# RWKV mixing: a PSUM copy of h as second operand of the mixes, and low parts of the key inputs by turns

## The chip, the cores and the metric

The kernel runs on one core of one Trainium2 chip. The metric is the device time of one execution in microseconds (us). PE is TensorE (matmuls), DVE is VectorE, ACT is ScalarE, POOL is GpSimd, SP is SyncE, which here only issues DMAs. SBUF is the working memory of the engines, PSUM the memory into which PE writes; DVE and ACT read and write both.

## What is computed

Two layers of a generator with 512 latent tokens and 256 context tokens of 1024 channels. Layer 0 mixes tokens by neighbourhood attention, layer 1 by bidirectional RWKV-7; each is followed by 16 experts. The change lies at the start of the RWKV layer, where every token's vector `h` is mixed with the mean of its two neighbours, with six learned vectors, one for each product that follows:

```
def centred_shift(h):
    hp = jnp.pad(h, ((0, 0), (1, 1), (0, 0)))
    return 0.5 * (hp[:, :-2] + hp[:, 2:])
xx = centred_shift(h) - h
x_s = h + xx * mix[s]          # s = receptance, decay, key, value, iclr, gate (0..5)
r, k, v = x_0 @ w_r, x_2 @ w_k, x_3 @ w_v
decay, iclr, gate: low-rank products, x_1 @ w1, x_4 @ a1, x_5 @ g1, each followed by a second one
```

(The last three lines are the reference's, shortened to their shape.)

## The kernel before

`rw_inputs` first norms the rows and turns them, so that channels lie on the 128 partitions: `hh` holds for each of 8 channel blocks `k` 772 columns (512 latent and 256 context tokens with zero columns between), all float32 in SBUF. A loop over the 8 blocks then does the mixing. For a block, `shifted(k)` makes `xx`: POOL adds the left and the right neighbour (`q` is POOL's queue, line 1069), DVE halves and subtracts `h` (line 1070). `mix(s, k)` makes one mixed input: one DVE instruction, `xx` times a column of `mixT` plus `h` (line 1079); or, with `spread`, a scaled copy on ACT and an add of `h` on POOL (lines 1076 and 1077). Six mixes are made for a block:

- 1 (decay) and 4 (iclr), 770 columns, for the low-rank products on PE (line 1117), whose sums lie in PSUM in `ph`;
- 2 (key), 770 columns: `part` splits it for the three-pass products into a rounded high part `xah` (ACT, line 947) and the rest `xal` (line 948, on POOL for blocks 0 to 6, on DVE for block 7);
- 5 (gate), 512 columns, for line 1119;
- 0 (receptance), 512 columns on DVE, and 3 (value), 770 columns by the spread way, tile name `md`; both go to DRAM (`xmd`, lines 1126 and 1127) and are loaded again later.

On the way PE also forms the keys of the first three token tiles (lines 1123 to 1125, sums in `pk`). Then `lora` and three copies empty the PSUM tiles on ACT and DVE, and a woven stage follows: products of keys and receptances on PE (lines 260 to 262) and `rw_keys`, then the values, then the scan over the tokens, then routing and the experts.

PSUM has 8 banks: 3 of the pool `mm`, 2 of `tp`, 3 of `ps_k0` here. The order of each engine's instructions in this part is set when the kernel is built, by a scheduler that plays the program through and takes the instructions as they come ready; each engine then runs its list strictly in order. The scan's order is written out by hand.

Of the kernel before, what the change touches and what calls it, by code (L numbers as in the profile page):

```python
# [20 lines left out]
F32 = mybir.dt.float32  # L21
# [984 lines left out]
def rw_inputs(S, pool):  # L1006

    nc, I, tc = S.nc, S.I, S.tc
    q = nc.gpsimd
# [15 lines left out]
    with tc.tile_pool(name="rwn", bufs=1) as xn:  # L1025
# [11 lines left out]
        hp = S.rwk.enter_context(tc.tile_pool(name="rwh", bufs=1, side="right"))  # L1037
# [28 lines left out]
    S.wraw = left.enter_context(tc.tile_pool(name="rwwr", bufs=2, reuse_waits="tile"))  # L1066

    def shifted(k):
        q.tensor_tensor(xx[:, k], hh[:, k, 0:770], hh[:, k, 2:772], op=ALU.add)
        nc.vector.scalar_tensor_tensor(xx[:, k], xx[:, k], 0.5, hh[:, k, 1:771], op0=ALU.mult, op1=ALU.subtract)  # L1070

    def mix(s, k, n=770, tag="mx", spread=False):
        t = wl.tile([P, 770], F32, name=tag, bufs=MXB[tag])[:, :n]
        m = mixT[:, 8 * s + k:8 * s + k + 1]
        if spread:
            nc.scalar.activation(t, xx[:, k, :n], AF.Copy, scale=m)
            q.tensor_tensor(t, t, hh[:, k, 1:n + 1], op=ALU.add)
        else:
            nc.vector.scalar_tensor_tensor(t, xx[:, k, :n], m, hh[:, k, 1:n + 1], op0=ALU.mult, op1=ALU.add)
        return t  # L1080

    def lora(ps, hid, fn):
        for z in range(2):
            for p, c0, n in ps:
                hs, h1 = (h[:, c0:c0 + n] for h in hid[z])
                t = wl.tile([64, 512], F32, name="ht")[:, :n]
                nc.scalar.activation(t, p[64 * z:64 * z + 64, :n], fn)
                nc.vector.tensor_copy(hs[0:64], t)
                nc.vector.tensor_copy(h1[0:64], t)
                nc.vector.tensor_tensor(hs[64:128], t, hs[0:64].bitcast(F32), op=ALU.subtract)  # L1090

    def weights(name, n):
        return split_weights(S, wp, "w", [(0, I[name][0][:, n * 256:(n + 1) * 256])], 3)

    xk = halves(xsp, "xa", 770)
    ready, S.ks = {}, [[None] * (NT // 2) for n in range(4)]
    with tc.tile_pool(name="rwl", bufs=2, reuse_waits="tile") as wl, tc.tile_pool(name="ps_k0", bufs=3, space=PSUM) as ps0:
        lw = []
        for name in ("rw_w1", "rw_a1"):
            w = wl.tile([P, KD, 2, 64], F32, name="lw", bufs=3)  # L1100
            for z in range(2):
                q.dma_start(w[:, :, z, :], I[name][0, z].rearrange("(k p) r -> p k r", p=P))
            lw.append(w.rearrange("p k z r -> p k (z r)"))
        lw.append(wl.tile([P, KD, P], F32, name="lw", bufs=3))
        q.dma_start(lw[2], I["rw_g1"][0].rearrange("(k p) r -> p k r", p=P))
        w0 = weights("rw_w_k", 0)
        ph = [[(p.tile([P, 512], F32, name=n), c0, w) for c0, w in ((0, 512), (512, 256))]
              for p, n in ((S.ps_tp, "tp"), (S.ps_mm, "mm"))]
        pg = S.ps_mm.tile([P, 512], F32, name="mm")
        pk = [ps0.tile([P, 256], F32, name="k0") for _ in range(3)]  # L1110
        for k in range(KD):
            shifted(k)
            on = dict(start=(k == 0), stop=(k == KD - 1))
            for i, s in enumerate((1, 4)):
                t = mix(s, k)
                for p, c0, n in ph[i]:
                    nc.tensor.matmul(p[:, :n], lw[i][:, k], t[:, at(c0 // P):at(c0 // P) + n], **on)
            part(S, xk, k, mix(2, k), q if k < LOQ else nc.vector)
            nc.tensor.matmul(pg, lw[2][:, k], mix(5, k, SEQ), **on)
            for t in range(3):  # L1120
                s = slice(t * P, (t + 1) * P)
                (xh, xl), (wh, wll) = (x[:, k, s] for x in xk), w0(k)
                nc.tensor.matmul(pk[t], xh, wh, start=(k == 0), stop=False)
                nc.tensor.matmul(pk[t], xh, wll, start=False, stop=False)
                nc.tensor.matmul(pk[t], xl, wh, start=False, stop=(k == KD - 1))
            nc.sync.dma_start(S.xmd[0][k], mix(0, k, SEQ, "md"))
            nc.sync.dma_start(S.xmd[1][k], mix(3, k, tag="md", spread=k < SPREAD))
        lora(ph[0], hidW, AF.Tanh)
        lora(ph[1], hidA, AF.Copy)
        nc.scalar.activation(S.hidG, pg, AF.Tanh, scale=0.5)  # L1130
        nc.vector.tensor_scalar(S.hidG, S.hidG, 0.5, 0.5, op0=ALU.mult, op1=ALU.add)
        base.close()
        S.kp = S.rwk.enter_context(tc.tile_pool(name="rwkst", bufs=2, side="right", reuse_waits="tile"))

        def key_tile(n, t):
            if t % 2 == 0:
                S.ks[n][t // 2] = S.kp.tile([P, 2, 256], F32, name="ks", bufs=KSB)
# [24 lines left out]


MXB = {"mx": 5, "md": 2}
SPREAD, LOQ, KSB, BOOST = 8, 7, 6, 1000
KSTART, KRATE = 0, 1.75


# [777 lines left out]
```

## Time and profile before

| | us |
|---|---|
| median of 3 runs | 2755.37 |
| their range | 2753.96 to 2766.93 |
| profiled execution, its own time | 2758.18 |
| its span, first to last instruction | 2756.4 |
| mixing loop in it, about | 1304 to 1374 |

Over the span PE is busy 90%, DVE 48%, ACT 36%, POOL 21%. These are means over stages with different limits: in the loop that the change touches DVE has next to no idle time, in the stages behind it PE is the busy one, and in the last third the loads of the experts' weights keep the DMA engines full. The page's chain that ended last follows those weights back through the last 320 us. So a reading of the loop must go by its own stretch. [...]

### The profile page before, as it was taken

The numbers are of one execution on the slowest core, as the hardware profiler recorded it, in microseconds if no ns is written. First come the engines' busy times: TensorE is split into PE (matmuls) and PEld (weight loads), VectorE is DVE, ScalarE is ACT, GpSimd is POOL, SyncE is SP. The second block draws the span as 40 slices with busy tenths as digits, with TensorE's granted clock in tenths as the row PEclk, the third lists the DMA queues.
The fourth block names the chain that finished last, engine by engine and source line by source line (L and its number), as shares of the span: only waits on it lengthen the run. The fifth ranks groups of instructions, "written<-read, shape, count | busy, mean of one in ns | idle before, by whom it ended". The sixth has DMA issues, their size and how long they took to land. (4 is left out here: it accounts for less than half of the span.)

```text
span 2756.4 us, 44025 instructions
## 1 busy us (share of the span) xinstructions
PE 2470.2 (90%) x16800; PEld 1574.1 (57%) x16800; DVE 1327.1 (48%) x3006; ACT 1004.0 (36%) x2127; POOL 591.5 (21%) x857
## 2 busy tenths in 40 slices
PE   6998999898999999997698697999999977998887
PEld 4876879793333333333388686777777862332222
DVE  6665566642222222225978845666666771221222
ACT  3555556642111101113266634766665431000100
POOL 2100000121000000001656525665655110000000
PEclk9999999998999999998899898999999978999999
DMA  8646440328787878784157866565554369999998
GB/s 246 147 150 187 132 152 15 109 100 327 298 320 312 334 305 329 293 357 172 69 186 241 269 167 130 124 134 125 126 122 125 87 243 378 420 420 421 420 420 342
DMA packets 378371, 637.64 MB, mean 231 GB/s; under 512 B 133832, under 2 KB 301056, under 8 KB 329008
## 3 DMA queue, kind: packets, MB, share of 16 engines
q1 hardware_dynamic: 370944, 609.11, 63.5%
q0 software_dynamic: 7216, 25.70, 2.5%
q8 instruction: 134, 2.20, 0.3%
q14 instruction: 77, 0.63, 0.1%
HBM read 565.11 MB, written 53.88 MB: 225 GB/s over the span
## 5 line engine op out<-in xcount | busy, mean ns | idle before, releaser
L790 PE MATMUL P<-wm,xin 128*64 128x512 f32 x2048 | 494.3, 601 | 25.8 <-DMA wm<-in_moe_w_dram 24.7
L790 PEld LDWEIGHTS P<-wm,xin 128*64 128x64 f32 x2048 | 141.0, 137 | 328.3 <-issue 259.4
L823 PE MATMUL mm<-wm,hidT 128*64 128x512 f32 x1024 | 245.9, 601 | 16.8 <-ACT hidT L807 14.9
L801 ACT ACTIVATE hid<-P 128x512 f32<-128x512 f32 x32 | 19.1, 597 | 563.3 <-PE P L790 563.3
L763 POOL DMA_INDIRECT xg<-xnd,ii x20 | 19.7, 985 | 846.5 <-PE tp L77 571.5
L837 DVE SCALAR_TENSOR_TENSOR Y<-mm,gates,gt 64x512 f32<-64x512 f32 x64 | 48.0, 750 | 283.1 <-PE mm L823 282.4
L260 PE MATMUL mm<-wh,hTh 128*128 128x256 f32 x576 | 173.5, 302 | 1.9 <-ACT hTh L554 1.9
L802 DVE TENSOR_TENSOR hid<-P,hid 128x512 f32<-128x512 f32 x32 | 22.1, 692 | 308.3 <-PE P L790 293.6
L262 PE MATMUL mm<-wh,hTl 128*128 128x256 f32 x576 | 168.4, 293 | 1.9 <-DVE hTl L557 1.9
L261 PE MATMUL mm<-wl,hTh 128*128 128x256 f32 x576 | 168.7, 293 | 0.0
L823 PEld LDWEIGHTS mm<-wm,hidT 128*64 128x64 f32 x1024 | 72.7, 137 | 151.9 <-issue 121.3
L1477 POOL TENSOR_TENSOR Wi<-Wi,Ti 112x30 f32<-112x30 f32 (+14 forms) x240 | 141.4, 589 | 18.8
L1475 POOL TENSOR_TENSOR Ti<-Wi 112x30 f32<-112x30 f32 (+14 forms) x240 | 134.9, 562 | 18.2
L795 PE MATMUL Pc<-wm,xin 128*32 128x512 f32 x1024 | 138.5, 597 | 0.0
L260 PEld LDWEIGHTS mm<-wh,hTh 128*128 128x128 f32 x576 | 114.3, 199 | 11.9 <-issue 8.8
L262 PEld LDWEIGHTS mm<-wh,hTl 128*128 128x128 f32 x576 | 113.6, 198 | 4.5 <-DVE hTl L557 2.8
L1554 PE MATMUL mm<-FR,QF 128*128 128x128 f32 (+1 forms) x768 | 115.1, 294 | 0.4 <-ACT QF L1542 0.4
L261 PEld LDWEIGHTS mm<-wl,hTh 128*128 128x128 f32 x576 | 114.6, 199 | 1.3 <-issue 1.1
L864 DVE TENSOR_TENSOR X<-mm,X 128x512 f32<-128x512 f32 x80 | 52.6, 687 | 111.9 <-PE mm L863 111.7
L1554 PEld LDWEIGHTS mm<-FR,QF 128*128 128x128 f32 x768 | 98.7, 200 | 7.4 <-ACT QF L1542 0.9
L1542 ACT ACTIVATE QF<-mm 64x256 f32<-64x256 f32 x192 | 72.6, 378 | 67.7 <-PE mm L1538 64.3
L1557 DVE TENSOR_TENSOR FT<-mm,eye 64x128 f32<-64x128 f32 x192 | 55.8, 292 | 78.9 <-ACT FT L1556 76.6
(437 smaller groups left out, 5715.6 us busy)
## 6 DMA issues: line engine op xcount, KB each, us to landing
wm<-in_moe_w_dram SPq DMA_DIRECT2D x378, 1024.0 KB
adaw<-in_ada_w_dram SPq DMA_DIRECT2D x96, 512.0 KB
wraw<-in_na_w_qkv_dram SPq DMA_DIRECT2D x32, 256.0 KB
wm<-in_moe_w_dram POOLq DMA_DIRECT2D x6, 1024.0 KB, 10.8
pkd<-sig SPq DMA_DIRECT2D x24, 256.0 KB
pkd<-kka SPq DMA_DIRECT2D x24, 256.0 KB
pkd<-av SPq DMA_DIRECT2D x24, 256.0 KB
sig<-pkd SPq DMA_DIRECT2D x16, 384.0 KB
```

What stands on the lines that cost most here:

```text
L260: S.nc.tensor.matmul(ps, xh, wh, start=(k == 0), stop=False)
L261: S.nc.tensor.matmul(ps, xh, wl, start=False, stop=False)
L262: S.nc.tensor.matmul(ps, xl, wh, start=False, stop=(k == n - 1))
L790: nc.tensor.matmul(ps[64 * hf:64 * hf + 64], xin[:, k, cl], w[:, hf * 512:(hf + 1) * 512], start=k == 0, stop=k == KD - 1)
L795: nc.tensor.matmul(Pc[32 * i:32 * i + 32], xinc[:, k, cc], ws[k][i // 2][:, (i % 2) * 512:(i % 2 + 1) * 512], start=k == 0, stop=k == KD - 1)
L823: nc.tensor.matmul(py[64 * hf:64 * hf + 64], hT[:, k % 4, k // 4, :], ws[k][:, hf * 512:(hf + 1) * 512], start=k == 0, stop=k == KD - 1)
L864: nc.vector.tensor_tensor(X[t][:, sl], ps, X[t][:, sl], op=ALU.add)
L1475: nc.gpsimd.tensor_tensor(t, W3[:, i + 1:32, i:i + 1].to_broadcast([112, n, i]), W3[:, i:i + 1, 0:i].to_broadcast([112, n, i]), op=ALU.mult)
L1477: nc.gpsimd.tensor_tensor(W3[:, i + 1:32, 0:i], W3[:, i + 1:32, 0:i], t, op=ALU.add)
L1542: nc.scalar.activation(QF[m][0:64, u], pq[64 * u:64 * u + 64], AF.Copy)
L1554: nc.tensor.matmul(pf[:, h, s0:], QF[m][:, u, h, :], rhs, start=True, stop=True)
L1557: nc.vector.tensor_tensor(F[64:128, :, 64:128], pf[64:128, :, 64:128], S.eye2[64:128, None, :].to_broadcast([64, 2, 64]), op=ALU.add)
```

## The change

For each block ACT copies `h` from `hh` to a PSUM tile `hp` (line 1072 of the changed kernel). DVE's subtract (line 1073) and its five mixes (line 1083) read `hp` in place of `hh`. The spread mix reads `hh` as before, and is now the first of a block. The low part `xal` is made on DVE for even blocks and on POOL for odd ones (line 1130).

To make room, `hp` takes 2 banks, and there is one such tile; `ps_k0` keeps one bank for one key tile. The other two key tiles share a bank of `mm`, and the two 256-column ends of the low-rank sums share a bank of `tp`; of the sums that share a bank only the first begins with `start`.

```diff
     def shifted(k):
+
         q.tensor_tensor(xx[:, k], hh[:, k, 0:770], hh[:, k, 2:772], op=ALU.add)
-        nc.vector.scalar_tensor_tensor(xx[:, k], xx[:, k], 0.5, hh[:, k, 1:771], op0=ALU.mult, op1=ALU.subtract)
-
-    def mix(s, k, n=770, tag="mx", spread=False):
+        hp = ps0.tile([P, 1024], F32, name="hp")[:, :770]
+        nc.scalar.activation(hp, hh[:, k, 1:771], AF.Copy)
+        nc.vector.scalar_tensor_tensor(xx[:, k], xx[:, k], 0.5, hp, op0=ALU.mult, op1=ALU.subtract)
+        return hp
+
+    def mix(s, k, hp, n=770, tag="mx", spread=False):
...
-            nc.vector.scalar_tensor_tensor(t, xx[:, k, :n], m, hh[:, k, 1:n + 1], op0=ALU.mult, op1=ALU.add)
+            nc.vector.scalar_tensor_tensor(t, xx[:, k, :n], m, hp[:, :n], op0=ALU.mult, op1=ALU.add)
...
-    with tc.tile_pool(name="rwl", bufs=2, reuse_waits="tile") as wl, tc.tile_pool(name="ps_k0", bufs=3, space=PSUM) as ps0:
+    with tc.tile_pool(name="rwl", bufs=2, reuse_waits="tile") as wl, tc.tile_pool(name="ps_k0", bufs=1, space=PSUM) as ps0:
...
-        ph = [[(p.tile([P, 512], F32, name=n), c0, w) for c0, w in ((0, 512), (512, 256))]
-              for p, n in ((S.ps_tp, "tp"), (S.ps_mm, "mm"))]
+        pc = S.ps_tp.tile([P, 2, 256], F32, name="tp")
+        ph = [[(S.ps_tp.tile([P, 512], F32, name="tp"), 0, 512), (pc[:, 0], 512, 256)],
+              [(S.ps_mm.tile([P, 512], F32, name="mm"), 0, 512), (pc[:, 1], 512, 256)]]
         pg = S.ps_mm.tile([P, 512], F32, name="mm")
-        pk = [ps0.tile([P, 256], F32, name="k0") for _ in range(3)]
+        pk = S.ps_mm.tile([P, 2, 256], F32, name="mm")
+        pk = [pk[:, 0], pk[:, 1], ps0.tile([P, 256], F32, name="k0")]
         for k in range(KD):
-            shifted(k)
+            hp = shifted(k)
...
+            nc.sync.dma_start(S.xmd[1][k], mix(3, k, hp, tag="md", spread=True))
...
-            part(S, xk, k, mix(2, k), q if k < LOQ else nc.vector)
-            nc.tensor.matmul(pg, lw[2][:, k], mix(5, k, SEQ), **on)
+            t = mix(2, k, hp)
+            nc.scalar.activation(xk[0][:, k], t, AF.Copy)
+            nc.tensor.matmul(pg, lw[2][:, k], mix(5, k, hp, SEQ), **on)
+            nc.sync.dma_start(S.xmd[0][k], mix(0, k, hp, SEQ, "md"))
+            (q if k % 2 else nc.vector).tensor_tensor(xk[1][:, k], t, xk[0][:, k].bitcast(F32), op=ALU.subtract)
...
-            nc.sync.dma_start(S.xmd[0][k], mix(0, k, SEQ, "md"))
-            nc.sync.dma_start(S.xmd[1][k], mix(3, k, tag="md", spread=k < SPREAD))
```

The scheduler gives the engines other lists with it. DVE's list at the loop's start, before, from the first `xx`: `xx` is a block's shift, `mx` and `md` are its mixes (`out<-in`, partitions x columns).

```order
L1070 SCALAR_TENSOR_TENSOR xx<-xx,hh 128x770
L253 TENSOR_TENSOR wl<-wraw,wh 128x1024
L1079 SCALAR_TENSOR_TENSOR mx<-xx,mixT,hh 128x770 x3
L1079 SCALAR_TENSOR_TENSOR mx<-xx,mixT,hh 128x512
L1079 SCALAR_TENSOR_TENSOR md<-xx,mixT,hh 128x512
L1070 SCALAR_TENSOR_TENSOR xx<-xx,hh 128x770 x4
L1079 SCALAR_TENSOR_TENSOR mx<-xx,mixT,hh 128x770 x2
L1079 SCALAR_TENSOR_TENSOR md<-xx,mixT,hh 128x512
```

And DVE's list of the change at the same place, through blocks 0, 1 and the first half of 2.

```order
L1073 SCALAR_TENSOR_TENSOR xx<-xx,hp 128x770
L253 TENSOR_TENSOR wl<-wraw,wh 128x1024
L1083 SCALAR_TENSOR_TENSOR mx<-xx,mixT,hp 128x770 x3
L1083 SCALAR_TENSOR_TENSOR mx<-xx,mixT,hp 128x512
L1083 SCALAR_TENSOR_TENSOR md<-xx,mixT,hp 128x512
L1130 TENSOR_TENSOR xal<-mx,xah 128x770
L1073 SCALAR_TENSOR_TENSOR xx<-xx,hp 128x770
L1083 SCALAR_TENSOR_TENSOR mx<-xx,mixT,hp 128x770 x3
L1083 SCALAR_TENSOR_TENSOR mx<-xx,mixT,hp 128x512
L1083 SCALAR_TENSOR_TENSOR md<-xx,mixT,hp 128x512
L1073 SCALAR_TENSOR_TENSOR xx<-xx,hp 128x770
```

The shifts no longer run ahead of the mixes: a block is now one shift and five mixes, and an even block has its low part behind them.

ACT's list in the loop, before (`md` the scaled copy of the spread mix, `xah` the high part of the key input):

```order
L1076 ACTIVATE md<-xx,mixT 128x770
L947 ACTIVATE xah<-mx 128x770
L1076 ACTIVATE md<-xx,mixT 128x770
L947 ACTIVATE xah<-mx 128x770
L1076 ACTIVATE md<-xx,mixT 128x770
```

And ACT's list of the change there:

```order
L1080 ACTIVATE md<-xx,mixT 128x770
L1127 ACTIVATE xah<-mx 128x770
L1072 ACTIVATE hp<-hh 128x770
L1080 ACTIVATE md<-xx,mixT 128x770
L1127 ACTIVATE xah<-mx 128x770
L1072 ACTIVATE hp<-hh 128x770
```

The copy `hp` of a block stands behind the scaled copy and the high part of the block before it.

The third place is ACT's list behind the loop, where the sums are emptied. Before (`ht` empties a low-rank sum, `hidG` the gate's, `ks` a key tile):

```order
L1087 ACTIVATE ht<-tp 64x512
L1130 ACTIVATE hidG<-mm 128x512
L1087 ACTIVATE ht<-tp 64x256
L1087 ACTIVATE ht<-mm 64x512
L1076 ACTIVATE md<-xx,mixT 128x770
L1087 ACTIVATE ht<-mm 64x256
L1087 ACTIVATE ht<-mm 64x512
L1087 ACTIVATE ht<-mm 64x256
L1140 ACTIVATE ks<-k_10871 128x256
```

And of the change, from the copies `w2s` of the next stage's weights on:

```order
L1230 ACTIVATE w2s<-wraw 64x1024 x2
L1139 ACTIVATE hidG<-mm 128x512
L1091 ACTIVATE ht<-tp 64x512
L1091 ACTIVATE ht<-tp 64x256
L1149 ACTIVATE ks<-mm 128x256 x2
L1149 ACTIVATE ks<-k_10871 128x256
L1220 ACTIVATE krows<-krows 128x256
L1234 ACTIVATE w_11357<-wraw 1x1024 x2
L1158 ACTIVATE ks<-mm 128x256
```

The key copies now come before the low-rank sums of the pool `mm`, and two copies of weights before `hidG`. Behind this stage the scan's lists are the same.

## Rows read from the trace of the kernel before

**Rows 1.** Stretches: us, busy PE, PEld, DVE, ACT, POOL (instructions); clock, DMA share, GB/s.

```profile
1304.00:1384.00 80.00, 50.78 (x181) 30.72 (x179) 78.49 (x71) 20.54 (x28) 48.77 (x23) 0.84 0.19 70
1384.00:1590.00 206.00, 171.26 (x1288) 165.05 (x1289) 158.92 (x205) 131.84 (x224) 114.68 (x114) 0.91 0.75 237
1590.00:2212.00 622.00, 571.84 (x4406) 488.14 (x4405) 402.73 (x1072) 358.41 (x891) 318.00 (x532) 0.95 0.55 124
2435.00:2756.00 321.00, 271.48 (x1170) 92.29 (x1168) 70.70 (x117) 27.07 (x53) 3.75 (x4) 0.99 0.97 404
```

**Rows 2.** Chain that ended last, its first long DMA piece: start, us, what.

```profile
2435.40 21.12 DMA wm<-in_moe_w_dram
```

**Rows 3.** Timeline, SP's issues of the last layer's expert weights: start, us, what.

```profile
2232.82 96.23 SPq L645 DMA_DIRECT2D wm<-in_moe_w_dram  x38
```

**Rows 4.** DVE's groups by shape, 1300 to 1376 us: busy us, mean ns.

```profile
L1079 DVE SCALAR_TENSOR_TENSOR mx<-xx,mixT,hh 128x770 f32<-128x770 f32 x24 | 37.9, 1615 | 0.0
L1070 DVE SCALAR_TENSOR_TENSOR xx<-xx,hh 128x770 f32<-128x770 f32 x8 | 11.0, 1417 | 0.0
L1079 DVE SCALAR_TENSOR_TENSOR md<-xx,mixT,hh 128x512 f32<-128x512 f32 x7 | 10.6, 1513 | 0.0
L1079 DVE SCALAR_TENSOR_TENSOR mx<-xx,mixT,hh 128x512 f32<-128x512 f32 x8 | 7.1, 890 | 0.0
```

**Rows 5.** Instructions that read or write `hh`: ns least/median/most, first and last start.

```profile
L1079 DVE SCALAR_TENSOR_TENSOR mx<-xx,mixT,hh x32: 736/1009/2591, 1310.0 to 1371.8; 128x770 f32<-128x770 f32 x24, 128x512 f32<-128x512 f32 x8
L1069 POOL TENSOR_TENSOR xx<-hh x8: 1459/2181/2447, 1303.8 to 1317.8; 128x770 f32<-128x770 f32 x8
L1070 DVE SCALAR_TENSOR_TENSOR xx<-xx,hh x8: 948/949/2558, 1305.9 to 1332.5; 128x770 f32<-128x770 f32 x8
```

**Rows 6.** DVE's timeline in the loop: start, us, what, idle before.

```profile
1329.12 1.01 DVE L1079 SCALAR_TENSOR_TENSOR mx<-xx,mixT,hh 128x770 f32<-128x770 f32 x1
1331.59 1.82 DVE L1070 SCALAR_TENSOR_TENSOR xx<-xx,hh 128x770 f32<-128x770 f32 x2
...
1372.83 0.96 DVE L948 TENSOR_TENSOR xal<-mx,xah 128x770 fp32r<-128x770 f32 x1 [0.25 <-ACT xah L947]
...
1377.89 0.73 DVE L1079 SCALAR_TENSOR_TENSOR md<-xx,mixT,hh 128x512 f32<-128x512 f32 x1
```

**Rows 7.** POOL's timeline at the loop's start.

```profile
1303.75 15.92 POOL L1069 TENSOR_TENSOR xx<-hh 128x770 f32<-128x770 f32 x8 [10.11 <-ACT hh L1063]
```

**Rows 8.** DVE adds with one operand in PSUM, near the scan's end: least/median/most.

```profile
L1715 DVE TENSOR_TENSOR acc<-mf,acc x64: 411/425/426, 2117.8 to 2229.2; 128x256 f32<-128x256 f32 x64
```

**Rows 9.** Timeline there, POOL and DVE at the same time.

```profile
2156.21 2.52 POOL L1694 TENSOR_TENSOR fraw<-fraw,rgate 128x512 f32<-128x512 f32 x2 [6.39 <-DMA fraw<-in_rw_w_o_dram]
2156.26 0.42 DVE L1715 TENSOR_TENSOR acc<-mf,acc 128x256 f32<-128x256 f32 x1 [0.61 <-PE mf L262]
...
2157.56 0.42 DVE L1715 TENSOR_TENSOR acc<-mf,acc 128x256 f32<-128x256 f32 x1 [0.60 <-PE mf L262]
```

**Rows 10.** A DVE instruction of the mixes' kind, `mm` in PSUM: busy us, mean ns.

```profile
L837 DVE SCALAR_TENSOR_TENSOR Y<-mm,gates,gt 64x512 f32<-64x512 f32 x64 | 48.0, 750 | 283.1 <-PE mm L823 282.4
```

**Rows 11.** ACT's groups, 1300 to 1376 us: busy us, mean ns, idle before.

```profile
L947 ACT ACTIVATE xah<-mx 128x770 fp32r<-128x770 f32 x8 | 6.8, 846 | 51.1 <-DVE mx L1079 51.1
L1076 ACT ACTIVATE md<-xx,mixT 128x770 f32<-128x770 f32 x7 | 6.5, 935 | 3.2 <-DMA xmd<-md 1.8 <-DVE xx L1070 1.4
```

**Rows 12.** PE's timeline behind the loop: start, us, what, idle before and its releaser.

```profile
1377.57 0.39 PE L260 MATMUL mm<-wh,xah 128*128 128x256 f32 x1 [2.74 <-ACT hidG L1130]
...
1385.37 0.58 PE L260 MATMUL mm<-wh,xah 128*128 128x256 f32 x1 [3.18 <-ACT ht L1087]
```

**Rows 13.** Timeline: SP's issue of two `xmd` stores, and ACT behind them.

```profile
1320.25 9.31 SPq L1126 DMA_DIRECT2D xmd<-md  x2
...
1331.32 0.94 ACT L1076 ACTIVATE md<-xx,mixT 128x770 f32<-128x770 f32 x1 [0.30 <-DMA xmd<-md]
```

**Rows 14.** ACT's timeline behind the loop, two copies of weights: start, us, what.

```profile
1387.16 2.14 ACT L1221 ACTIVATE w2s<-wraw 64x1024 fp32r<-64x1024 f32 x2
```

More of the change, by code (lines that the diff above doesn't have):

```diff
@@ L1106, in rw_inputs @@
         w0 = weights("rw_w_k", 0)
-        ph = [[(p.tile([P, 512], F32, name=n), c0, w) for c0, w in ((0, 512), (512, 256))]
-              for p, n in ((S.ps_tp, "tp"), (S.ps_mm, "mm"))]
+        pc = S.ps_tp.tile([P, 2, 256], F32, name="tp")
+        ph = [[(S.ps_tp.tile([P, 512], F32, name="tp"), 0, 512), (pc[:, 0], 512, 256)],
+              [(S.ps_mm.tile([P, 512], F32, name="mm"), 0, 512), (pc[:, 1], 512, 256)]]
         pg = S.ps_mm.tile([P, 512], F32, name="mm")
-        pk = [ps0.tile([P, 256], F32, name="k0") for _ in range(3)]
+        pk = S.ps_mm.tile([P, 2, 256], F32, name="mm")
+        pk = [pk[:, 0], pk[:, 1], ps0.tile([P, 256], F32, name="k0")]
         for k in range(KD):
-            shifted(k)
+            hp = shifted(k)
             on = dict(start=(k == 0), stop=(k == KD - 1))
+            nc.sync.dma_start(S.xmd[1][k], mix(3, k, hp, tag="md", spread=True))
             for i, s in enumerate((1, 4)):
-                t = mix(s, k)
+                t = mix(s, k, hp)
                 for p, c0, n in ph[i]:
-                    nc.tensor.matmul(p[:, :n], lw[i][:, k], t[:, at(c0 // P):at(c0 // P) + n], **on)
-            part(S, xk, k, mix(2, k), q if k < LOQ else nc.vector)
-            nc.tensor.matmul(pg, lw[2][:, k], mix(5, k, SEQ), **on)
+                    nc.tensor.matmul(p[:, :n], lw[i][:, k], t[:, at(c0 // P):at(c0 // P) + n],
+                                     start=k == 0 and (i == 0 or c0 == 0), stop=k == KD - 1 and (i == 1 or c0 == 0))
+            t = mix(2, k, hp)
[3 more added lines that the diff above has]
+            (q if k % 2 else nc.vector).tensor_tensor(xk[1][:, k], t, xk[0][:, k].bitcast(F32), op=ALU.subtract)
             for t in range(3):
@@ L1122, in rw_inputs @@
                 (xh, xl), (wh, wll) = (x[:, k, s] for x in xk), w0(k)
-                nc.tensor.matmul(pk[t], xh, wh, start=(k == 0), stop=False)
+                nc.tensor.matmul(pk[t], xh, wh, start=(k == 0 and t != 1), stop=False)
                 nc.tensor.matmul(pk[t], xh, wll, start=False, stop=False)
-                nc.tensor.matmul(pk[t], xl, wh, start=False, stop=(k == KD - 1))
-            nc.sync.dma_start(S.xmd[0][k], mix(0, k, SEQ, "md"))
-            nc.sync.dma_start(S.xmd[1][k], mix(3, k, tag="md", spread=k < SPREAD))
+                nc.tensor.matmul(pk[t], xl, wh, start=False, stop=(k == KD - 1 and t > 0))
         lora(ph[0], hidW, AF.Tanh)
@@ L1164 @@
 MXB = {"mx": 5, "md": 2}
-SPREAD, LOQ, KSB, BOOST = 8, 7, 6, 1000
+KSB, BOOST = 6, 1000
 KSTART, KRATE = 0, 1.75
```

## The prediction

> **What bounds the kernel now.** I read the stretches first, since the page's shares mix stages. In 1304 to 1384 us DVE is busy 78.5 of 80 us, and PE, ACT and POOL are not near that [rows 1]: the mixing loop is DVE's. Behind it PE is busy 171 of 206 and 572 of 622 us, and in the last 321 us the DMA share is 0.97 [rows 1]; the chain that ended last runs there through the loads of expert weights [rows 2]. That does not make the loop worthless: SP begins that stream only at 2232.8 us, when the RWKV layer ends [rows 3], so whatever ends the loop sooner moves the stream with it, unless a stage between gives the time back.
>
> Then DVE's own instructions. A 770-column mix takes 1.01 us when nothing disturbs it, a shift 0.95, a 512-column mix 0.74 [rows 5, 6], but in the loop the means are 1.6 us for the 24 mixes of 770 columns, 1.4 for the shifts and 1.5 for `md` [rows 4]. The stretched ones, up to 2.6 us, lie beside POOL's adds, which are themselves slower than their least time of 1.46 us (median 2.18) [rows 5]; in the first 16 us POOL adds without a break [rows 7]. All of these DVE instructions have two operands in SBUF. An add with one operand in PSUM keeps its price beside POOL: two of 0.42 us lie inside one 2.5 us stretch of POOL's [rows 9], and all 64 of that line take 411 to 426 ns [rows 8]. So the stretch belongs to the second SBUF operand.
>
> **The change part by part.**
>
> The stretch. DVE's 48 shifts and mixes take 37.9 + 11.0 + 10.6 + 7.1 us [rows 4] and 0.7 for the eighth `md` [rows 6], 67.3 in all. Alone they would take 24 x 1.01 + 8 x 0.95 + 16 x 0.74 = 43.7. With `hp` in PSUM the difference goes: -23.6 us. The bound on the other side is nothing gained.
>
> The PSUM operand itself. The nearest row is an instruction of the same kind with one operand in PSUM, 512 columns: 750 ns [rows 10], against 736 for ours from SBUF [rows 5]. 14 ns x 48 is +0.7 us. [...] The row of this trace is for 64 partitions, but of the same length; I go by it.
>
> Low parts on DVE. Four in place of one: three more, at 0.96 us alone [rows 6]: +2.9. They keep two SBUF operands; that of block 0 falls into POOL's eight sums and may take twice as long: +1.0. The others meet POOL idle or at the end of an add, since POOL loses three low parts and its adds should come near 1.46 us; bounds 0 to +3 more.
>
> The copy `hp`. No row shows ACT writing PSUM. The nearest is its 770-column copy within SBUF, 0.85 us [rows 11]; I take that, bounds 0.6 and 1.1. ACT has the room, 20.5 of 80 us busy [rows 1]. But there is one `hp`: the copy of the next block can only begin when `md`, the last mix, has read it, and DVE's next shift waits for it. Behind an even block DVE has its low part meanwhile (0.96 us, about the copy and its semaphores), so nothing is lost. Behind blocks 1, 3 and 5 DVE stands for 0.95 us each: +2.9 (bounds 2 to 4). In ACT's list the copy stands behind `xah` and `md` of the block before; `xah` is done about 0.5 us before the last mix ends, so it doesn't hold the copy.
>
> The first store. `md` has two buffers, and the spread mix of block 0 waits for its add on POOL behind the eight sums. These end at 1319.7 us now [rows 7], at about 1316.5 if each takes 1.5. Add, store and about 2.1 us until it has landed (second issue at 1329.2, ACT released at 1331.3 [rows 13]) make the buffer free at 1320.5; by the sum below DVE wants it at 1320.2. I take +0.5, bounds 0 and 4.
>
> The sum for the loop: -23.6 + 0.7 + 2.9 + 1.0 + 2.9 + 0.5 = -15.6 us. Checked by blocks: an even or odd block is 0.98 + 3 x 0.95 + 0.68 + 0.75 us (starts overlap by some 0.07 [rows 6]) and 0.95 for the low part or the wait, 6.2 us; the first two blocks end at 1322.6, five more take 31, and the last 5.3: 1358.9 us. Before, the last low part ended at 1373.8, and one `md` was still to come [rows 6]. So the loop ends 14.9 us earlier with that `md` done.
>
> Handover to PE. Before, PE's next products began at 1377.6, 3.8 us behind the loop, and stood again for 3.2 us until `ht` had emptied a bank [rows 12]. In the new list `hidG` stands behind the last high part and two weight copies of 2.1 us together [rows 14] and takes 0.6: about 4.2 us behind the loop, so +0.4. The second bank comes from the key copies right behind it, sooner than PE's first product is done; the 3.2 us could go altogether, but ACT then waits for `krows`, a load that is issued late, and PE's third product for ACT. I take half of it: -1.5, bounds 0 and -3.2.
>
> What follows has the same work. PE's waits for `rw_keys` stay as a whole; its list and the loads of receptance inputs are dealt anew, which I cannot cost: 0, bounds -6 and +8. The scan's lists are the same. PE's clock in the loop was 0.84 [rows 1]; a shorter loop has less idle time for PE, so I add nothing for it.
>
> **The sum:** -14.9 + 0.4 - 1.5 = -16.0 us. The profiled execution took 2758.18 us, 1.8 beyond its span and 2.8 over the median of the runs, so it gives 2742.2 of its kind and 2739.4 as a median.
>
> **The rivals.**
>
> (a) The woven stage gives part of it back. For it: the scheduler placed the loads of receptance inputs and their high parts later, and ACT waits for `krows` between the key copies; PE has 35 us of idle time there already [rows 1], so the stage hangs on chains and not on PE alone. Against: these chains begin with the keys, which come earlier. A loss of 8 leaves 8 gained: 2747.
>
> (b) The ring of `md` buffers sets the pace. The scaled copy (0.94), POOL's add (2.0 if still stretched), an odd low part ahead of it (2.0) and the store (2.5) make 7.4 us, with semaphores about 7.7, against my 6.2; ACT's list then holds `hp` as well. 1.5 x 7 is 10 us: gain 6, 2749. Against: POOL's adds have fewer DVE instructions to fight, and the low part of an odd block stands only in every second round. It decides from a round over 6.2 us.
>
> (c) Slower: the PSUM operand doesn't free DVE, because it is the running `xx` in SBUF and the write that POOL holds up. Then the 23.6 us stay, three more low parts at the loop's stretched 1.4 us, the waits for `hp` and 0.7 come on top: +8, 2763. Decided at once by the mean of a mix in the loop: 1.6 us again. Against stand all 64 adds of [rows 8], in which one SBUF operand and an SBUF write are there too.
>
> (d) The copy isn't used as meant: DVE's list shows `hp` in all six instructions of a block, so no chance is kept for that.
>
> **How the numbers follow.** Forecast 0.62, with a spread of some 6 us either way from the unknown costs (2733 to 2746); (a) 0.22; (b) 0.11; (c) 0.05. About 0.5%, 13.8 us, is what a measurement of this kernel can tell from no change: the line lies at 2741.6, just above the forecast. Of the forecast's chance the larger part is below it, since the open terms (the 3.2 us, PE's clock, POOL's faster adds) lean to more gain: 0.50, and 0.02 from (a); slower by as much only if (c) or a loss behind the loop is larger than costed, 0.03. Range 2731 to 2753: it leaves out the far side of (b), all of (c), and gains over 24 us.
>
> **What would show it.** Right: the means of DVE's 770-column mixes fall to 1.0 us and of the shifts to 0.95; a gap of about 1 us before each shift of blocks 2, 4 and 6 with `hp` as its releaser; the low parts at 0.96 except the first; the loop's last mix near 1359; PE's first product of line 260 near 1363; the stretch from there to the first weights of the experts as long as before within some us. Wrong: mixes over 1.3 us (c); `md` on ACT or DVE waiting for the store in most blocks (b); a loop that ends at 1359 and a scan that begins less than 10 us earlier (a).

## The result and the profile after

The changed kernel took 2739.77 us (median of 6 runs, 2729.94 to 2747.81), the kernel before beside it 2759.18 (6 runs, 2753.96 to 2766.93): a ratio of 0.9926, 95% interval 0.9898 to 0.9954. The forecast was 2739.4, 16.0 us less than before. Run again twice beside the kernel before, it gave 0.9932 (0.9906 to 0.9959) and 0.9940 (0.9919 to 0.9960). Over all runs the mean is 2759.9 before (43 runs) and 2741.2 after (17 runs), 18.7 us less, give or take 2.8.

The profiled execution of the changed kernel took 2747.81 us, its slowest; so the gain is read by stages, from POOL's first sum in each trace, since what lies ahead of it has the same lists. Three stretches: the loop up to PE's first product of line 260; the woven stage up to ACT's last copy `rkv` of a product out of PSUM; the scan up to the first add into `XB`, which holds the layer's result. First the kernel before (us, busy PE, PEld, DVE, ACT, POOL with instructions; then the granted clock, which is the mean share of PE's full speed in the stretch, DMA share, GB/s).

```profile
1303.75:1377.57 73.82, 46.42 (x159) 26.56 (x157) 72.53 (x58) 18.72 (x24) 47.47 (x22) 0.84 0.18 68
1377.57:1665.55 287.98, 246.56 (x1849) 236.96 (x1850) 202.52 (x290) 164.33 (x288) 142.07 (x157) 0.92 0.70 210
1665.55:2238.35 572.80, 520.14 (x3977) 435.16 (x3975) 384.81 (x1050) 334.57 (x847) 298.22 (x500) 0.94 0.52 120
```

The same three in the changed kernel:

```profile
1300.70:1359.27 58.57, 44.41 (x158) 27.18 (x156) 50.78 (x64) 27.78 (x34) 31.88 (x20) 0.86 0.27 104
1359.27:1653.90 294.63, 246.52 (x1849) 235.22 (x1850) 206.16 (x288) 162.22 (x286) 143.86 (x160) 0.91 0.68 202
1653.90:2225.30 571.40, 526.42 (x3977) 439.36 (x3975) 383.43 (x1050) 335.21 (x847) 294.56 (x495) 0.93 0.53 120
```

The loop is 15.25 us shorter, the woven stage 6.65 longer, the scan 1.4 shorter; further executions, below, tell how much of the last two is chance. What happened in the loop, DVE's groups of the changed kernel (busy us, mean ns, idle before and its releaser), to be held against [rows 4]:

```profile
L1083 DVE SCALAR_TENSOR_TENSOR mx<-xx,mixT,hp 128x770 f32<-128x770 f32 x24 | 23.0, 1012 | 0.6
L1073 DVE SCALAR_TENSOR_TENSOR xx<-xx,hp 128x770 f32<-128x770 f32 x8 | 7.6, 956 | 3.2 <-ACT hp L1072 3.1
L1083 DVE SCALAR_TENSOR_TENSOR md<-xx,mixT,hp 128x512 f32<-128x512 f32 x8 | 5.9, 742 | 3.9 <-DMA xmd<-md 3.9
L1083 DVE SCALAR_TENSOR_TENSOR mx<-xx,mixT,hp 128x512 f32<-128x512 f32 x8 | 5.9, 741 | 0.0
L1130 DVE TENSOR_TENSOR xal<-mx,xah 128x770 fp32r<-128x770 f32 x4 | 3.8, 961 | 0.0
```

The 48 shifts and mixes take 42.4 us where they took 67.3. A 770-column mix is 1.01 us in the mean, as an undisturbed one was before [rows 6]. POOL gains as well: its sums and the copies in ACT (ns least, median, most; first and last start):

```profile
L1070 POOL TENSOR_TENSOR xx<-hh x8: 1458/1467/2535, 1300.7 to 1312.7; 128x770 f32<-128x770 f32 x8
L1081 POOL TENSOR_TENSOR md<-md,hh x8: 1545/1548/1552, 1314.1 to 1353.2; 128x770 f32<-128x770 f32 x8
L1072 ACT ACTIVATE hp<-hh x8: 813/817/818, 1300.9 to 1350.3; 128x770 f32<-128x770 f32 x8
```

The new waits of DVE, from its timeline (start, us, what, idle before and its releaser):

```profile
1308.95 0.98 DVE L1130 TENSOR_TENSOR xal<-mx,xah 128x770 fp32r<-128x770 f32 x1
...
1311.04 3.53 DVE L1083 SCALAR_TENSOR_TENSOR mx<-xx,mixT,hp 128x770 f32<-128x770 f32 x4
1318.50 0.75 DVE L1083 SCALAR_TENSOR_TENSOR md<-xx,mixT,hp 128x512 f32<-128x512 f32 x1 [3.93 <-DMA xmd<-md]
1320.13 0.96 DVE L1073 SCALAR_TENSOR_TENSOR xx<-xx,hp 128x770 f32<-128x770 f32 x1 [0.88 <-ACT hp L1072]
...
1332.46 0.96 DVE L1073 SCALAR_TENSOR_TENSOR xx<-xx,hp 128x770 f32<-128x770 f32 x1 [0.94 <-ACT hp L1072]
...
1338.92 0.96 DVE L1073 SCALAR_TENSOR_TENSOR xx<-xx,hp 128x770 f32<-128x770 f32 x1 [0.35 <-ACT hp L1072]
...
1345.06 0.96 DVE L1073 SCALAR_TENSOR_TENSOR xx<-xx,hp 128x770 f32<-128x770 f32 x1 [0.88 <-ACT hp L1072]
```

The last mix ends 55.7 us after POOL's first sum; before, the last low part ended at 70.0 with an `md` to come. And PE behind the loop, which answers [rows 12], with the longest wait of the woven stage below it:

```profile
1359.27 0.39 PE L260 MATMUL mm<-wh,xah 128*128 128x256 f32 x1 [0.80 <-ACT hidG L1139]
...
1366.99 0.39 PE L260 MATMUL mm<-wh,xah 128*128 128x256 f32 x1 [1.70 <-ACT ks L1158]
...
1548.35 1.01 PE L260 MATMUL mm<-wh,xvh 128*128 128x256 f32 x3 [9.59 <-ACT wh L252]
```

### The profile page after: what moved, and what is told of

Its sections match the earlier page's. It is cut to its first block, busy times and chain, and to the rows that moved or that the text cites. A ratio compares the mean times of both kernels' runs of the same rounds, so it can differ in the third digit from the quotient of the medians.

```text
span 2745.7 us, 44024 instructions
## 1 busy us (share of the span) xinstructions
PE 2475.8 (90%) x16800; PEld 1578.2 (57%) x16800; DVE 1308.1 (48%) x3009; ACT 1011.5 (37%) x2135; POOL 574.1 (21%) x854
## 5 line engine op out<-in xcount | busy, mean ns | idle before, releaser
L823 PE MATMUL mm<-wm,hidT 128*64 128x512 f32 x1024 | 245.7, 601 | 16.7 <-ACT hidT L807 14.9
L260 PE MATMUL mm<-wh,hTh 128*128 128x256 f32 x576 | 172.5, 300 | 1.9 <-ACT hTh L554 1.9
L802 DVE TENSOR_TENSOR hid<-P,hid 128x512 f32<-128x512 f32 x32 | 22.1, 692 | 309.5 <-PE P L790 295.1
L260 PEld LDWEIGHTS mm<-wh,hTh 128*128 128x128 f32 x576 | 113.4, 197 | 12.0 <-issue 8.8
```

The source lines that it names most:

```text
L260: S.nc.tensor.matmul(ps, xh, wh, start=(k == 0), stop=False)
L823: nc.tensor.matmul(py[64 * hf:64 * hf + 64], hT[:, k % 4, k // 4, :], ws[k][:, hf * 512:(hf + 1) * 512], start=k == 0, stop=k == KD - 1)
```

## The experiments

The theory: the stretch of DVE's instructions beside POOL comes from the second SBUF operand, and `hp` in PSUM takes it away. Rival: something else in the change (the order of the list, fewer low parts on POOL) does it. For the time behind the loop: the woven stage gives some back by its new list, or not.

**The operand alone (r1), with the change repeated beside it (r4).** The kernel before, measured together with these two, took 2760.91 us. The edit of r1 to the changed kernel:

```diff
-            nc.vector.scalar_tensor_tensor(t, xx[:, k, :n], m, hp[:, :n], op0=ALU.mult, op1=ALU.add)
+            nc.vector.scalar_tensor_tensor(t, xx[:, k, :n], m, hh[:, k, 1:n + 1], op0=ALU.mult, op1=ALU.add)
```

> The changed kernel with one thing undone: the five mixes of a block read h from SBUF again; the shift still reads the PSUM copy, so the copy, its waits and the bank layout stay. Theory (a second SBUF operand is stretched by POOL): the 770-column mixes go from 1.01 us back to a mean of 1.4 to 1.7, the loop from POOL's first sum to DVE's last mix from 55.7 us to 68 to 76, and the time comes to 2750 to 2762, near the kernel before. Rival (the gain came from DVE's new list, which no longer runs shifts ahead, and from the banks): mixes stay at 1.0 to 1.1 us, the loop at 56 to 59, the time at 2740.

> The changed kernel again, for its second profile. If the list sets it: the loop takes 55.7 us again within 0.5, DVE waits 3.9 us for the first store's buffer, and PE stands 9 to 10 us before the first value product because the copy of the value weights stands on ACT behind a high part that waits for DVE. If these were accidents of one execution, they differ by several us.

Measured: r1 2750.16 us (6 runs), r4 2741.49 (5 runs). DVE's groups of r1 in the loop:

```profile
L1083 DVE SCALAR_TENSOR_TENSOR mx<-xx,mixT,hh 128x770 f32<-128x770 f32 x24 | 34.3, 1466 | 0.0
L1083 DVE SCALAR_TENSOR_TENSOR md<-xx,mixT,hh 128x512 f32<-128x512 f32 x8 | 10.5, 1312 | 0.0
L1073 DVE SCALAR_TENSOR_TENSOR xx<-xx,hp 128x770 f32<-128x770 f32 x8 | 7.6, 944 | 0.0
L1130 DVE TENSOR_TENSOR xal<-mx,xah 128x770 fp32r<-128x770 f32 x4 | 5.5, 1388 | 0.0
```

One of its shifts lies inside one of POOL's sums:

```profile
1311.80 1.91 POOL L1070 TENSOR_TENSOR xx<-hh 128x770 f32<-128x770 f32 x1
1312.30 0.94 DVE L1073 SCALAR_TENSOR_TENSOR xx<-xx,hp 128x770 f32<-128x770 f32 x1
```

With their second operand back in SBUF the mixes stretch again to 1.47 us in the mean, and so do two of the four low parts, which have two SBUF operands; the shifts, which still read `hp`, stay at 0.94 in the same loop. So the operand decides about the stretch. The scheduler dealt r1's list anew as well, but one list holds both kinds here; and fewer low parts on POOL are not the reason either, as r2 below gives three back to POOL and its mixes stay at 1.01 us.

What the operand is worth in time is less plain. The 48 shifts and mixes take 59.5 us in r1, 17.1 of the 24.9 us that the change took off, and the last mix ends at 72.8 us, within the 68 to 76 expected. But PE's first product of line 260 comes at 63.8 us, only some 5 later than in the changed kernel and 10 earlier than before: DVE's waits for the store and for `hp`, 7 us in the changed kernel, are gone in r1, and two receptance mixes fall behind the loop. The time is 8.7 us over r4's, give or take some 8 with so few runs, of the changed kernel's 19.4 under before; the rest came with the shift's operand, the other list and fewer low parts on POOL, which this run leaves in and no run parts. r4 repeats what it was to repeat: the last mix at 56.2 us, a wait of 4.5 us for the first store, and 9.58 us of PE's wait in the woven stage.

**POOL idle (r3).** The kernel before, without the add of `h` in the spread mix and with all low parts on DVE, so that POOL has only the eight sums. It leaves out that `h` from the value input.

```diff
-            q.tensor_tensor(t, t, hh[:, k, 1:n + 1], op=ALU.add)
...
-SPREAD, LOQ, KSB, BOOST = 8, 7, 6, 1000
+SPREAD, LOQ, KSB, BOOST = 8, 0, 6, 1000
```

> The kernel before, with POOL emptied behind its first eight sums: the low parts all on DVE, and the add of h in the spread mix left out (the value inputs are then only the scaled difference, so the output is another). All mixes keep two SBUF operands. Theory (only POOL stretches them): once the sums are done, some 16 us into the loop, every 770-column mix takes 1.01 us, every low part 0.96; mixes over 1.3 us stand only beside the sums. Rival (two SBUF operands are slow here for another reason, PE's or ACT's reads among them): the later mixes still show 1.4 us and more.

Its timeline, POOL's sums and DVE beside and behind them:

```profile
1300.07 15.92 POOL L1069 TENSOR_TENSOR xx<-hh 128x770 f32<-128x770 f32 x8 [10.01 <-ACT hh L1063]
```

```profile
1306.28 8.38 DVE L1078 SCALAR_TENSOR_TENSOR mx<-xx,mixT,hh 128x770 f32<-128x770 f32 x4
...
1323.34 1.01 DVE L1078 SCALAR_TENSOR_TENSOR mx<-xx,mixT,hh 128x770 f32<-128x770 f32 x1
```

Beside the sums four mixes take 8.38 us; from their end at 1316.0 on, with both operands still in SBUF, each takes 1.0. So in these loops both were needed, POOL at work and two operands in SBUF: 2.1 us a mix where both hold, 1.0 here with POOL idle and 1.01 in the changed kernel with `hp`. (2741.31 us, one run.)

Both together are not enough, though. In the changed kernel two instructions of DVE with two SBUF operands fall into POOL's sums and are not stretched, a piece `wl` of the weights and the low part of block 0 (1308.95, above). Here `wl` before and in the changed kernel, and POOL's sum beside that low part:

```profile
1307.56 2.48 DVE L253 TENSOR_TENSOR wl<-wraw,wh 128x1024 fp32r<-128x1024 f32 x1
```

```profile
1303.72 1.22 DVE L253 TENSOR_TENSOR wl<-wraw,wh 128x1024 fp32r<-128x1024 f32 x1
...
1309.08 2.18 POOL L1070 TENSOR_TENSOR xx<-hh 128x770 f32<-128x770 f32 x1
```

In both cases DVE began first, by 0.01 and 0.13 us, and the sum that POOL then began took 2.54 and 2.18 us in place of 1.47. Before, `wl` began 0.8 us behind a sum and took twice its time. So where the two met, the price fell on POOL as well as on DVE: 0.7 to 1.1 us of POOL's in the changed kernel, 1.3 of DVE's before. The order of the starts may decide it; that is not shown, as no run varied it.

**The turns (r2, r8).** r2 gives POOL the low parts of blocks 0 to 6, r8 gives DVE all eight:

```diff
-            (q if k % 2 else nc.vector).tensor_tensor(xk[1][:, k], t, xk[0][:, k].bitcast(F32), op=ALU.subtract)
+            (q if k < 7 else nc.vector).tensor_tensor(xk[1][:, k], t, xk[0][:, k].bitcast(F32), op=ALU.subtract)
```

> The changed kernel with the low parts of blocks 0 to 6 on POOL again, so without the turns. Theory (on even blocks the low part runs while DVE would wait for the copy of the next block): DVE saves three low parts of 0.96 us and waits 0.9 us more behind blocks 0, 2, 4 and 6; the loop stays within 2 us of 55.7 and the time within 6 us of the changed kernel. Rival (each low part on DVE lies on the path): the loop is 3 to 4 us shorter, and the time too.

> The changed kernel with the low parts of the key inputs on VectorE in all eight blocks where it takes turns with GpSimd: four more of 0.96 us on VectorE, 3.85 us. Theory: VectorE waits some 3 us in the loop for ACT's copy of the next block, behind the blocks that hold a low part least, and the added work falls partly into these waits and into the wait for the first store, so the last mix ends 56 to 58 us after GpSimd's first sum and the time is within 2 us of the changed kernel on this chip. Rival (VectorE has no idle time that it can use): 3.9 us later, at 59.6, and the time 4 us longer.

In r2 the last mix ends 55.3 us after the first sum: DVE has four low parts, 3.8 us, less to do before it (the one that it keeps comes behind) and waits 6.4 us for `hp`, in 7 waits, instead of 3.1 in 4. In r8 it ends at 56.1 with three low parts, 3.5 us, more to do before it; the wait for the store falls to 2.54 us, those for `hp` to 1.2 in all. So the turns are worth nothing in the loop: DVE's low part and its wait for `hp` stand in for each other. The times are 2747.40 (4 runs) and 2745.08 (4 runs), 5.9 and 3.6 us over the changed kernel (r2 by r4, measured with it, r8 by the median of all 17 runs). For r8 that misses the 2 us that were expected. Their loops don't show why; their woven stages, 299.3 and 298.0 us, are longer than the changed kernel's 294.6 to 297.3.

**A third buffer for `md` (r5).**

```diff
-MXB = {"mx": 5, "md": 2}
+MXB = {"mx": 5, "md": 3}
```

> The changed kernel with three buffers for the decay mixes of the first loop where it has two, so that VectorE's third decay mix need not wait for the first store (it waited 3.93 us there in the changed kernel's execution, 4.5 in its repetition). Theory: that wait goes and no other takes its place, so the last mix ends about 52 us after GpSimd's first sum instead of 55.7, and PE's first matmul of L260 comes some 4 us earlier from there; the time falls by 4 us from that of the changed kernel on this chip, or by less if the stage behind takes it back as it took back 7. Rival (the store is late because of GpSimd's eight sums, and with a third buffer the fourth mix waits instead): the wait moves to the next decay mix and the last mix stays at 55 to 56 us.

```profile
1314.48 0.74 DVE L1083 SCALAR_TENSOR_TENSOR md<-xx,mixT,hp 128x512 f32<-128x512 f32 x1
1316.19 0.96 DVE L1073 SCALAR_TENSOR_TENSOR xx<-xx,hp 128x770 f32<-128x770 f32 x1 [0.96 <-ACT hp L1072]
```

The wait for the store is gone and no `md` waits after it; the last mix ends at 51.45 us, PE's first product of line 260 comes at 54.4 instead of 58.6. The time is 2735.99 us (4 runs), against 2762.15 of the kernel before beside it (ratio 0.9908, 0.9891 to 0.9925), and 5 us under the mean of the changed kernel's runs elsewhere. The theory held.

**The woven stage (r9, r12, r6, r10).** In the changed kernel PE waits 9.59 us for ACT's copy of the first value weights (line 252), which stands in ACT's list behind two copies that wait for DVE:

```profile
1544.19 0.42 ACT L1262 ACTIVATE hk<-kkb 128x256 f32<-128x256 f32 x1 [4.16 <-DVE kkb L1259]
1546.93 0.42 ACT L1262 ACTIVATE hk<-kkb 128x256 f32<-128x256 f32 x1 [2.33 <-DVE kka L1266]
1547.26 1.04 ACT L252 ACTIVATE wh<-wraw 128x1024 fp32r<-128x1024 f32 x1
```

r6 loads and splits these weights earlier in the changed kernel, r10 the same in the kernel before; r9 and r12 are the kernel before and the changed one once more, for further traces of the stages.

```diff
+    S.tc.cur_priority -= VBOOST[0]
+    wv0 = split_weights(S, vp, "w", [(0, S.I["rw_w_v"][0][:, 0:256])], 2)
+    S.tc.cur_priority += VBOOST[0]
...
-        for _ in ahead_of(S, tokens(S, xv, vp, "rw_w_v", n, S.vd, NT, bonus, bufs=2), VBOOST[1 + n]):
+        for _ in ahead_of(S, tokens(S, xv, vp, "rw_w_v", n, S.vd, NT, bonus, bufs=2, w=wv0 if n == 0 else None), VBOOST[1 + n]):
```

> The changed kernel with the first 256 columns of the value weights loaded and split ahead of where they stood, so that ACT's copies at L252 stand in its list before the copies of the keys' low parts (L1262) that wait for VectorE. Theory: the changed kernel gives back 7 us in the stage woven with stage 0 because those copies come late (PE waited 9.59 us there for ACT's wh, 9.6 in the repetition); with them early that wait is under 2 us, the stretch from the first matmul of L260 to the last rkv is 288 to 291 us as in the kernel before instead of 295 to 296, and the time falls by 3 to 9 us from that of the changed kernel on this chip. Rival (PE's wait only shows that the whole stage is bound by ACT and VectorE): the wait shows up at another tile, the stretch stays at 294 us or more and the time within 2 us.

> The kernel before once more, for a second trace of it. Theory: the stretch from PE's first L260 matmul to the last rkv, 288.0 us in its first trace, is 286 to 291 us again, so that the 294 to 296 us of the changed kernel are its list's doing; the scan behind it may be anything from 561 to 577 us, and goes with the granted clock in it. Rival: the stretch is 293 us or more here, and the changed kernel's woven stage gave nothing back.

> The kernel before with the first value weights early, as in the run r6 of the changed kernel. Theory: the kernel before has waits of 0.6 to 1.95 us there, not 9.6, so the edit has nothing to give it: time within 2 us of before, stretch from the first L260 to the last rkv 286 to 291 us. Rival (the edit helps whatever the list ahead): 3 to 5 us faster than before, and what it gave the changed kernel is no part of what the change lost.

> The changed kernel a third time, to be compared with the two before it on the same chip: 13 us under the kernel before at an equal granted clock, by a line through all runs so far (time falls 1.43 us for each 0.001 of the span's granted clock), and 16 to 20 us in the medians.

Woven stage and scan of r9 (before), then of r12 (changed):

```profile
1374.59:1665.70 291.11, 248.69 (x1849) 238.42 (x1850) 201.12 (x290) 163.97 (x287) 140.61 (x157) 0.91 0.71 208
1665.70:2245.70 580.00, 526.86 (x3977) 440.76 (x3976) 382.89 (x1049) 334.95 (x847) 297.07 (x500) 0.92 0.51 118
```

```profile
1360.20:1657.50 297.30, 249.06 (x1848) 237.32 (x1849) 206.21 (x288) 161.49 (x285) 143.81 (x160) 0.90 0.68 200
1657.50:2224.00 566.50, 518.09 (x3977) 432.35 (x3976) 382.21 (x1049) 334.56 (x847) 297.79 (x495) 0.95 0.53 121
```

r9's woven stage, from one execution of 2765.53 us, lies at the end of what was expected, 286 to 291 us, and r12's shows the changed kernel's longer one a third time (2742.04 us, 6 runs, 15.4 under the kernel before beside it, just short of the 16 to 20 expected; at an equal clock, by the slope that was put down with it, 14 where 13 were expected). Scans with the same lists differ by up to 18 us, and within each kernel those with the higher granted clock are shorter: 572.8 us at 0.94 against 580.0 at 0.92 before, 561.8 and 566.5 at 0.95 against 571.4 at 0.93 in the change. So I took the clock out, by an estimate from the same traces: each stage cut into stretches of about 4 us, the time lost being (1 - granted clock) times the stretch, and summed. In us:

| kernel (trace) | loop, to first L260 | woven | lost to clock in it | the rest | scan | lost | the rest |
|---|---|---|---|---|---|---|---|
| before, first | 73.8 | 288.0 | 22.1 | 265.9 | 572.8 | 35.9 | 536.9 |
| before, r9 | 73.8 | 291.1 | 25.6 | 265.5 | 580.0 | 44.4 | 535.6 |
| changed, first | 58.6 | 294.6 | 27.2 | 267.4 | 571.4 | 41.1 | 530.3 |
| changed, r4 | 59.1 | 296.1 | 27.3 | 268.8 | 561.8 | 26.4 | 535.4 |
| changed, r12 | 59.3 | 297.3 | 30.7 | 266.6 | 566.5 | 29.9 | 536.6 |
| r6 | 58.7 | 289.7 | 23.8 | 265.8 | 577.1 | 43.1 | 534.0 |
| r10 | 73.8 | 282.1 | 23.9 | 258.2 | 584.0 | 35.0 | 549.0 |

The woven stage is 6.5 us longer in the change by the means (289.5 and 296.0); 4.5 of that is time lost to the clock, 1.9 the rest. But the clock's part can't be set apart from the list as chance. In all 14 traces the clock falls 145 to 158 us behind the first product of line 260, and how long it stays low goes with the kernel. The 50 us from 148 us behind that product on, before, changed, and in r6 (columns as above, the clock behind POOL's):

```profile
1525.57:1575.57 50.00, 28.79 (x165) 25.76 (x165) 43.67 (x59) 30.68 (x51) 28.38 (x31) 0.73 0.92 301
```

```profile
1507.27:1557.27 50.00, 22.12 (x98) 17.92 (x99) 41.71 (x54) 31.29 (x50) 27.64 (x31) 0.59 0.84 277
```

```profile
1507.03:1557.03 50.00, 29.70 (x160) 26.30 (x160) 42.51 (x57) 31.39 (x51) 29.52 (x31) 0.66 0.87 287
```

The same 50 us have 0.69 in r9, and 0.56 in r4 and r12: that is 13.5 and 15.5 us lost before, and 20.5 to 22 in the change. The wait of 9.59 us lies in them. So the new list may be behind all of the 6.5 us, and no run parts its waits from the clock.

In r6 PE's long wait is gone and the stage takes 289.7 us, 6.3 less, of which 4.6 is clock and 1.8 the rest: there the theory held. But the time, 2743.17 (6 runs, 2732.05 to 2751.52), is no better than the changed kernel's 2741.5, as the rival had it; the scan of r6's execution lost 43.1 us to the clock, more than any of the changed kernel's, and its runs spread too far to tell a gain of a few us from none. In r10, in its one trace and with the clock taken out, the woven stage takes 7.5 us less and the scan 12.8 more, and the time is 2756.41 us (10 runs) beside 2757.44 before (ratio 0.9988, 0.9971 to 1.0005). Its expected stretch of 286 to 291 us was missed; its time was not.

**Both edits (r7, r11): a version that beats both kernels.** The changed kernel with the edits of r5 and r6:

> The changed kernel with both of the edits before this: three buffers for the decay mixes, value weights of the first columns early. Theory: the two are in different stages and add up, some 7 to 12 us under the changed kernel on this chip, about 2730 us. Rival (what is won in the loop is waited away in the woven stage): no faster than the better of the two alone.

> The changed kernel with three decay buffers and the value weights early, again, to narrow its time: 8 to 10 us under the changed kernel of the same chip if the two add up (2729.81 us were measured where the kernel before took 2762.15), 3 to 4 if the second edit is lost again behind the first.

2729.81 us (4 runs) where the kernel before took 2762.15, and 2730.73 (6 runs) where it took 2757.44 and the changed kernel 2742.04; ratios to before 0.9901 (0.9870 to 0.9932) and 0.9899 (0.9879 to 0.9920). Of the 11 us under the changed kernel, more than the 8 to 10 expected, 4.9 are there at PE's first product of line 260 (54.3 us after the first sum in r11, 59.3 in r12). With the clock taken out, woven stage and scan together take 800.6 (r7) and 800.4 us (r11), against 800.8 in r5 alone and 797.7, 804.2 and 803.2 in the changed kernel, so what the second edit adds to the first is not seen in these stages; that is left open.

## Why the prediction came out as it did

**The cause and the rows for it were right.** That the second SBUF operand makes the stretch was read from the PSUM adds of [rows 8, 9]; r1 and r3 show it with the kernel's own mixes. Rival (c) fell with the first mean, 1.01 us.

**The loop, term by term.** In us:

| term | predicted | measured |
|---|---|---|
| stretch and PSUM operand | -22.9 | -24.9 |
| three more low parts on DVE | +2.9 | +2.9 |
| the one of block 0, stretched | +1.0 | 0 (0.98 us) |
| waits for `hp` | +2.9 | +3.1 |
| first store | +0.5 | +3.9 |
| last mix | -14.9 | -14.4 |
| first product of L260 | -14.5 | -15.2, in r4 and r12 -14.7 and -14.5 |

The price of the PSUM operand was set at 14 ns from [rows 10]; it is 3 ns for 770 columns (1.012 us against 1.009) and 5 for 512 (741 against 736), so the second operand in PSUM costs these instructions next to nothing. The rest of the 2.0 us in the first term is a slip of mine: I took a sum of single durations, 43.7, from a busy time, 67.3, in which overlapping ends count once. The low part of block 0 kept its 0.98 us; POOL's sum beside it took longer instead, as shown above.

**The step that was mis-sized is the first store.** I had POOL's sums end 12.75 us after their start, the buffer come free at 16.75 and DVE want it at 16.45. The sums took 13.4, two of them being the long ones beside DVE's two-operand instructions, and the store landed 2.85 us after its issue instead of 2.1, so that DVE's `md` started at 17.8; and DVE was there at 13.9, as block 0 had no stretched low part and `wl` ahead of it took 1.22 us in place of 2.48, which the sum had left out. POOL's sums and the `md` adds behind them, then SP's issue of their stores:

```profile
1300.70 13.42 POOL L1070 TENSOR_TENSOR xx<-hh 128x770 f32<-128x770 f32 x8 [10.12 <-ACT hh L1063]
1314.08 3.05 POOL L1081 TENSOR_TENSOR md<-md,hh 128x770 f32<-128x770 f32 x2
```

```profile
1315.65 1.82 SPq L1120 DMA_DIRECT2D xmd<-md  x2
```

The bound of 4 was nearly reached, and passed in r4 with 4.48. It is a matter of one buffer: r5 takes the wait away and 4.2 us at PE with it.

**The handover.** I had 4.2 us between the last mix and PE's product; it was 2.9, as the last high part on ACT was done before the last mix ended and only the two weight copies and `hidG` stood behind. PE's second wait is 1.70 us, as half of 3.2 was assumed.

**Behind the loop.** Rival (a) had its mark in the profile, a scan that begins less than 10 us earlier: 353.2 us after the first sum where it was 361.8. By stages it is half right: the woven stage took 6.5 us more, near its bound of 8, about 2 of it with the clock taken out and the rest in a clock that stays low longer beside the new list's waits, and the scan was shorter by 10 in the means (576.4 and 566.6), of which the clock is 7.7. Woven stage and scan together take 860.8 and 871.1 us before, and 857.9 to 866.0 in the change; with the clock taken out 802 in both (means 801.9 and 801.7). So zero was the right value for what follows, within that spread, but partly by luck: a longer woven stage and a shorter scan cancel.

**The time itself** was hit closer than the steps deserve. The base, 2755.37, was a median of three runs; with the next three it is 2759.18, and over 43 runs 2760.4. And the gain was 19.4 us in the medians of those first runs and 18.7 in the means of all, not 16.0. Two misses of some 4 and 3 us cancel. The 3 us beyond the loop go with the clock: over the runs for which it is known, the granted clock of the span is 0.9483 in the mean before and 0.9513 in the change, which by the 1.43 us for each 0.001 that r12 goes by is some 4 us. A part of that is the loop itself, in which (1 - clock) times the length falls from 11.8 us to 8.2. Whether the rest belongs to the change (a clock that falls less often in its scan) or to chance, two and three traces can't tell; that stays open.

Rival (b) did not decide: DVE's blocks took 6.14 to 6.46 us (from shift to shift, 1320.13 to 1345.06), near the 6.2 of the sum, and after the first `md` none waited for the ring.

## What to carry to other kernels

When DVE and GpSimd work side by side, look at the spread of one and the same DVE instruction: undisturbed ones far under the mean (1.01 us against 1.6 here), with GpSimd busy beside the long ones, and a DVE line with a PSUM operand that doesn't spread (411 to 426 ns), pointed here to the second SBUF operand; a copy of the common operand into PSUM by an idle ACT can then pay for itself, as it did here with eight copies of 0.82 us for 24.9 us of DVE's time. A single tile that every block needs brought its own short waits (0.35 to 0.94 us, 3.1 in all), and moving a small piece of work onto DVE or off it changed nothing in this loop (last mix at 56.1 and 55.3 us, against 55.7). Before a loss or gain behind the change is explained by a list, look at two executions of the same kernel and at the granted clock, stretch by stretch. Put down to chance what the clock took only where its falls move from one execution to the next; a fall that stands at the same place each time, longer with one list than with the other (13.5 and 15.5 us lost before, 20.5 to 22 in the change), points to the list.

## What was not expected of the hardware

The spread of this kernel's time, 17 us before and 23 after from the lowest to the highest run, goes for the most part with PE's clock: the more of it a run was granted, the shorter it was, with a correlation of -0.80 over 37 runs before and -0.86 over 17 after. In the traces the scan is where the executions of one kernel differ most, by 7.2 us before and 9.6 in the change, the woven stage by 3.1 and 2.7. In the changed kernel's trace the granted clock falls from 1.00 to 0.50 and comes back, here once more with the stretches around it (columns as above):

```profile
1770.00:1774.00 4.00, 3.54 (x38) 3.33 (x37) 2.57 (x8) 3.88 (x13) 3.53 (x7) 1.00 0.55 125
1774.00:1778.00 4.00, 3.31 (x21) 2.39 (x19) 2.66 (x5) 1.83 (x6) 3.65 (x5) 0.56 0.59 126
1778.00:1782.00 4.00, 4.00 (x16) 2.91 (x14) 0.59 (x2) 1.69 (x5) 3.49 (x7) 0.50 0.65 121
1782.00:1786.00 4.00, 4.00 (x19) 3.14 (x19) 1.85 (x5) 0.64 (x3) 3.36 (x9) 0.50 0.51 158
1786.00:1790.00 4.00, 4.00 (x27) 3.65 (x27) 3.33 (x5) 3.86 (x8) 3.71 (x4) 0.73 0.32 91
...
1842.00:1846.00 4.00, 2.71 (x22) 2.01 (x23) 3.08 (x5) 2.61 (x8) 3.69 (x5) 1.00 0.62 131
```

Ahead of the fall PE had three short waits:

```profile
1773.68 0.49 PE L1547 MATMUL mm<-RHS,TB 128*128 128x128 f32 x2 [0.46 <-ACT TB L1524]
1774.36 0.69 PE L1547 MATMUL mm<-RHS,TB 128*128 128x128 f32 x2 [0.19 <-ACT TB L1524]
1775.55 0.69 PE L1580 MATMUL ch<-Z,FT 128*64 128x64 f32 x4 [0.50 <-DVE Z L1583]
```

This fall loses 6.8 us ((1 - clock) times 4 us, summed). A longer gap in PE's work (1842 to 1846, 2.71 of 4 us busy) brought none, so these rows give no rule for when. There were 7 to 10 falls in the scans of the five traces of before and after, and the losses of 26 to 44 us go with the scans' lengths; the rests differ by 6.6 us at most.

ACT writes 770 float32 columns into PSUM in 0.817 us, against 0.846 for its rounded copy of as many columns within SBUF, so the copy that the change adds is no dearer than that one.
